# A weight stream with five raw buffers instead of four, smaller tile pools, and three kinds of work pinned to their places in the order

## The chip, the cores and the metric

The kernel runs on one core of one Trainium2 chip. A core has TensorE (PE in the profile; its weight loads are PEld), VectorE (DVE), ScalarE (ACT), GpSimd (POOL) and SyncE (SP), which each take their own instructions in order and wait for each other by semaphores. DMAs are issued from SyncE, GpSimd and ScalarE and run on 16 DMA engines. The metric is device microseconds of one execution. The kernel before takes 915.2 us (median of three, 913.45 to 915.28).

## The reference

One layer of a hybrid transformer block for 512 latent tokens of width 1024, with 256 context tokens as a prefix, all in float32. What it computes, cut to what matters here:

```python
sh1, sc1, g1, sh2, sc2, g2 = split(silu(c) @ w_ada + b_ada, 6)      # modulation from c
hx = rms_norm(x, norm1_g) * (1 + sc1) + sh1
u, vs, q, r, ga, gb, k, v, lr = split(hx @ w_in, IN_SPLITS)
a  = spatial_gating(gelu(u), gelu(vs), ...)                          # 8 groups of 128x128 over chunks of tokens
o  = gla_bidir(q, k, v, lr, ..., states of the context)              # chunked linear attention, 4 heads, 2 directions
ob = rms_norm per head(o) * gla_norm_g * silu(r)
merged = sigmoid(ga) * (a @ w_br_a) + sigmoid(gb) * (ob @ w_br_b)
x  = x + g1 * (merged @ w_o)
hx2 = rms_norm(x, norm2_g) * (1 + sc2) + sh2
a, val = split(hx2 @ w_up, 2)
x  = x + g2 * ((gelu(depthwise_conv3x3(a) + b) * val) @ w_down)
return rms_norm(x, final_norm_g)
```

`r`, `ga`, `gb` and the products with `w_br_a`, `w_br_b` and `w_o` are 512x1024 by 1024x1024.

## The kernel before, in words

**Arithmetic.** A float32 product is made of three products of rounded parts: a weight `raw` is loaded from HBM (512 KB, L238, SyncE), its rounded part `wh` is a copy on ScalarE (L250) and the rest `wl = raw - wh` a subtraction on VectorE (L251). Activations are split in the same way. TensorE then runs `wh` by the high part, `wh` by the low part and `wl` by the high part into one sum.

**The weight stream.** All big weights are pieces of one list, `specs`, used in order by `weights()`. Each use splits up to two pieces ahead (`stream_split(i + 2)`) and loads up to `AHEAD` pieces beyond that one (`stream_load(i + 1 + AHEAD)`). `raw` tiles rotate through `RAW` buffers. A load waits until the `wl` subtraction that read its buffer last is done. `wh` and `wl` have five buffers each, and ScalarE waits for the matmuls that read them last.

**The gate stage.** The three gates and the product with `w_br_a` (`gate`, `gate_product`, L1347) compute a 2x2 block product with seven products instead of eight; each product takes two pieces of the stream and 24 matmuls. Some of the pieces are sums or differences of weight quarters. These sums are made in HBM by GpSimd: `sums_build` issues copies (L215) and accumulating DMAs (L217), one step per `next()`; the `hook()` of the heads and the context products advance it. Each such DMA depends on `after`, the last instruction traced before it, of whatever engine.

**The modulation vectors** `g1`, `sh2`, `sc2`, `g2` come late and by VectorE: `ada2` loads 256 KB pieces of `w_ada` (L1200, SyncE, tiles `wa` of one pool) and adds each, scaled by one element of silu(c) per partition, into `acc` (L1204). Each set is a generator in `bg`; `tick()` advances it at the places that the list `ticks` gives. The loads run `ahead` pieces before the additions.

**The operands of the w_br_a product.** `a_prep` loads eight quarters of the spatial-gating output back from HBM (16 DMAs on SyncE, L1442, tiles `aq`) and makes seven operands, each split by ScalarE (L1448) and VectorE (L1449); `a_step(n)` advances it n steps. `ob_step` does the like for the operand of `w_br_b`.

**What sets the order.** The code is traced in the order it is written, and a scheduler then puts each engine's instructions in an order of its own from its costs and from priorities, within data dependencies and buffer reuse. `in_order(start, engines...)` overrides this: it chains the instructions traced since `start` on the named engines in the order traced. `behind_last(f, engines...)` runs `f()` and chains what it traced behind the instruction of that engine that was traced last; in the kernel before it is used in the channel mixer only. Tiles come from pools: `late` (`LATE` slots of 2 KB per partition), `heap` (`HEAP` slots), and `wp` for the weight stream; a tile in a reused slot waits for the last reader of the one before.

Of the kernel before, what the change touches and what calls it, by code (L numbers as in the profile page):

```python
# [13 lines left out]
ALU = mybir.AluOpType  # L14
AX = mybir.AxisListType

P = 128
# [7 lines left out]
GW = 64  # L25
EPS = 1e-6
O_U, O_VS, O_Q, O_R, O_GA, O_GB, O_K, O_V, O_LR = 0, 1024, 2048, 2560, 3584, 4608, 5632, 6144, 7168
HEAP = 44
LATE = 27
AHEAD = 3  # L30
BLOCKS = 5
TAIL = FT - 4 * BLOCKS
LEAD = 5
# [1 line left out]
SUMS0 = 84  # L35
# [1 line left out]
DENSE = 10  # L37
SHSC = 6
WT = (1, 1)
RAW = 4  # L40


@with_exitstack
def backbone_kernel(
# [7 lines left out]
    V, A, G, T = nc.vector, nc.scalar, nc.gpsimd, nc.tensor  # L52

    cp = stack.enter_context(tc.tile_pool(name="cp", bufs=1))
    wp = stack.enter_context(tc.tile_pool(name="wp", bufs=5))
    hp = stack.enter_context(tc.tile_pool(name="hp", bufs=HEAP))
    lp = stack.enter_context(tc.tile_pool(name="lp", bufs=LATE))
# [11 lines left out]
    def heap(shape, dt=F32, s="h"):  # L69
        return hp.tile(shape, dt, tag="h", name=nm(s))  # L70

    def late(shape, dt=F32, s="l"):
        return lp.tile(shape, dt, tag="l", name=nm(s))
# [13 lines left out]
    dma = nc.sync.dma_start  # L87

    def traced():
        return nc.cur_bb.bb.instructions  # L90

    def in_order(start, *engines):

        last = {}
        for i in traced()[start:]:
            e = i.engine
            if e in engines:
                if e in last:
                    tc.add_manual_dep(i, last[e], mybir.DependencyInfo(
                        mybir.DependencyClass.NoSync, mybir.DependencyReason.DATA), reason="in_order")  # L100
                last[e] = i.name
# [56 lines left out]
    R_AT = len(specs)  # L158
# [17 lines left out]
    quarter, sums = quarters(ffn_w_down[0], 0), sum_tiles(BLOCKS)  # L176
# [29 lines left out]
    def sums_build(quarter, sums):  # L206
        for step in (((0, (0, 1)), (1, (1, 1)), (2, (1, 0)), (3, (0, 1))), ((0, (0, 0)), (3, (1, 1))),
                     ((1, 0),), ((2, 1),)):
            for b in range(len(sums)):
                for dst, src in step:  # L210
                    ap = quarter(b, *src) if isinstance(src, tuple) else sums[b][src]
                    after = traced()[-1]
                    start = len(traced())
                    if len(step) == 4:
                        G.dma_start(sums[b][dst], ap)  # L215
                    else:
                        G.dma_start(sums[b][dst], ap, accum_op=ALU.add)  # L217
                    for i in traced()[start:]:
                        if i.engine == G.engine:
                            tc.add_manual_dep(i, after.name, mybir.DependencyInfo(  # L220
                                mybir.DependencyClass.Sync, mybir.DependencyReason.SCHED_ONLY), reason="sums_build")
                    yield

    def gate_sums():
        for z in gate_weights:
            yield from sums_build(*z)

    building = [(SUMS0, sums_build(quarter, sums)), (2, gate_sums())]

    raws, splits = {}, {}  # L230
    pos = [0, 0, 0]
# [123 lines left out]
    cin = tok_load(ctx[0], 2, late)  # L355
    in_order(START, nc.sync.engine)


    bg = []

# [89 lines left out]
    cs = const([P, KT, 32], "cs")  # L450
# [303 lines left out]
    for k in range(1, KT):  # L754
        g = max(i for i in range(NG) if G0[i] <= k)
# [255 lines left out]
    hooked = [0]  # L1011

    def hook():
        hooked[0] += 1
        if hooked[0] % 2 and 2 < pos[2] < R_AT:
            next(building[1][1], None)
        if hooks:
            f = hooks.pop(0)
            f[0](*f[1:])
# [54 lines left out]
    for t in range(2):  # L1074
        ps = mm()
        for k in range(KT):
            wh, wl = fv[k // 2][1:]
            ah, al = hc[k]
            for i, (a, b) in enumerate(((ah, wh), (ah, wl), (al, wh))):
                T.matmul(ps, a[:, t * P:(t + 1) * P], b[:, k % 2, :], start=(k == 0 and i == 0),  # L1080
                         stop=(k == KT - 1 and i == 2))
            if t and k % 2:
                next(building[1][1])
        v_out(4 + t, ps)
        if t == 0:
            lrp = gl()
            for k0 in (0, 4):
                lr_part(lrp[:, :LC], fc, k0)
            lsc = heap([P, LC], s="lsc")
            A.copy(lsc, lrp[:, :LC])  # L1090
# [25 lines left out]

    ones_r = const([P, P], "ones_r", F32R)
    V.tensor_copy(ones_r, ones)
    sw = [late([P, 4, P], s="sw") for _ in range(2)]
    swT = [heap([P, 4, P], s="swT") for _ in range(2)]  # L1120
    for i in range(2):
        dma(sw[i], sgu_w[0, 4 * i:4 * i + 4].rearrange("g p q -> p g q"))
    sgb = [heap([P, 4, P], s="sgb") for _ in range(2)]
    for i in range(2):
        dma(sgb[i], sgu_b[0:1, 4 * i:4 * i + 4, :].rearrange("o g p -> o (g p)").to_broadcast([P, 512]))

    def sgu_turn(i):
        ps = gl()
        for g in range(4):
            T.transpose(ps[:, g * P:(g + 1) * P], sw[i][:, g, :], ident)  # L1130
        V.tensor_copy(swT[i], ps)

        sgu_hl.append(split_act(swT[i].rearrange("p g q -> p (g q)"), s="sw", lo_pool=late, hi_pool=late, eng=A.copy))
# [18 lines left out]
    def vs_done(hf, t, ps):  # L1152
        vraw[hf][t] = (late if hf else heap)([P, 512], s="vr")
        A.activation(vraw[hf][t], ps, AF.Gelu)

        for h_, t_ in ((), ((), ((0, 0), (0, 1), (1, 0), (1, 1)), ((0, 2), (0, 3), (1, 2)), ((1, 3),))[t])[hf]:
            V.bn_stats(stats[:, t_, h_, :], vraw[h_][t_])
        if hf and t == 0:
            behind.append(len(traced()))
        if hf and t == 1:  # L1160
            in_order(behind.pop(), V.engine)
# [13 lines left out]
    for hf in range(2):  # L1175
        for t in range(4):
            z = vraw[hf][t]
# [6 lines left out]
    def ada2(*kinds, ahead=ADA2):  # L1184
        todo = [(kind, j) for kind in kinds for j in range(2)]
        at = lambda kind, j: 2048 + ("g1", "sh", "sc", "g2").index(kind) * 1024 + j * 512
        acc = []
        for kind, j in todo:
            a_ = late([P, 512], s="acc")
            A.mul(a_.rearrange("p (b r) -> p b r", b=4), ident.unsqueeze(1).to_broadcast([P, 4, P]), 0.0)  # L1190
            c0 = at(kind, j)
            dma(a_[0:1, :], b_ada[0:1, c0:c0 + 512])
            acc.append(a_)
        coming, steps_ = [], [(k, i) for k in range(KT) for i in range(len(todo))]
        for n in range(len(steps_) + ahead):
            if n < len(steps_):
                k, i = steps_[n]
                c0 = at(*todo[i])
                w_ = late([P, 512], s="wa2")
                dma(w_, w_ada[0, k * P:(k + 1) * P, c0:c0 + 512])  # L1200
                coming.append(w_)
            if n >= ahead:
                k, i = steps_[n - ahead]
                V.scalar_tensor_tensor(acc[i], coming.pop(0), cs[:, k, 0:1], acc[i], op0=ALU.mult, op1=ALU.add)  # L1204
            yield
        pairs = []
        for a_ in acc:
            pairs.append(split_act(a_, s="acc", eng=A.copy))
            yield
        yield  # L1210
        yield
        for (ah, al), (kind, j) in zip(pairs, todo):
            ps = gl()
            T.matmul(ps, ones_r, ah, start=True, stop=False)
            T.matmul(ps, ones_r, al, start=False, stop=True)
            if kind in ("g1", "g2"):
                t_ = late([P, 512], s=kind)
                A.copy(t_, ps)
                bc_g[kind, j] = t_
            else:  # L1220
                t_ = heap([P, 4, P], s="dg")
                V.tensor_tensor(t_, ps.rearrange("p (b r) -> p b r", b=4),
                                ident.unsqueeze(1).to_broadcast([P, 4, P]), op=ALU.mult)
                if kind not in cols:
                    cols[kind] = const([P, 8], "col_" + kind)
                V.reduce_sum(cols[kind][:, j * 4:j * 4 + 4], t_, axis=AX.X)
            yield
# [245 lines left out]
    a_steps = a_prep()  # L1473

    def a_step(n):
        for _ in range(n):
            next(a_steps, None)

    ob, ob_step = restores(ob_kept, "ob")

# [9 lines left out]

    def bra_step(i):
        a_step((2, 0, 0, 0, 0, 0, 0)[i])
        if i > 3:
            ob_step()

    a_sum = of_sums(lambda name, b: found.pop((name, b)))
# [287 lines left out]

    n, todo = [0], []

    def behind_last(f, *engines):
        ends = [max(i for i, z in enumerate(traced()) if z.engine == e.engine) for e in engines]
        f()
        for e, i in zip(engines, ends):  # L1790
            in_order(i, e.engine)

    def product_in(ps, t, c0, n_, z, first, last):
        (wh, wl), (ah, al) = z
        for kk in range(2):
# [76 lines left out]
    ends = []  # L1872
# [42 lines left out]
```

## Time and profile before

| | us |
|---|---|
| median of three runs | 915.2 |
| the profiled execution | 916.71 |
| its span | 915.0 |
| TensorE busy | 897.1 (98%) |
| VectorE busy | 716.5 (78%) |
| ScalarE busy | 466.1 (51%) |
| GpSimd busy | 94.1 (10%) |
| one cast of a weight, L250 (178 of them) | 1.052 |
| one subtraction, L251 (178) | 1.220 |
| one modulation addition, L1204 (64) | 0.748 |

The profiled execution took 916.71 us from outside; its span, on which all times of the trace are counted, is 915.0. TensorE is busy almost throughout, so the table says where the others have room, and only a view in order of time says where TensorE waits. In the timeline a row has the start, the length, the engine, the line, the operation and the tiles (out<-in); "x2" merges two. In the chain of waits a row has the start, the length and what the end of the program was waiting for in that time.

### The profile page before, as it was taken

The numbers are of one execution on the slowest core, as the hardware profiler recorded it, in microseconds if no ns is written. First come the engines' busy times: TensorE is split into PE (matmuls) and PEld (weight loads), VectorE is DVE, ScalarE is ACT, GpSimd is POOL, SyncE is SP. The second block draws the span as 40 slices with busy tenths as digits, with TensorE's granted clock in tenths as the row PEclk, the third lists the DMA queues.
The fourth block names the chain that finished last, engine by engine and source line by source line (L and its number), as shares of the span: only waits on it lengthen the run. The fifth ranks groups of instructions, "written<-read, shape, count | busy, mean of one in ns | idle before, by whom it ended". The sixth has DMA issues, their size and how long they took to land.

```text
span 915.0 us, 12469 instructions
## 1 busy us (share of the span) xinstructions
PE 897.1 (98%) x4476; PEld 745.6 (81%) x4476; DVE 716.5 (78%) x1195; ACT 466.1 (51%) x768; POOL 94.1 (10%) x146
## 2 busy tenths in 40 slices
PE   7999999999999999999999999999999999999996
PEld 5778888888888877887888889888888888888885
DVE  5478687779785567659898767898899988986996
ACT  6356465657542636668541537443333434366663
POOL 1300012122112210000000000021111000000000
PEclk9999999999999999999999999999999999999999
DMA  9973677899797999895997850899998632355542
GB/s 284 335 249 117 204 159 134 245 275 249 158 271 250 312 275 310 282 302 180 365 390 263 287 179 24 247 264 275 209 209 199 139 94 95 119 173 187 168 155 92
DMA packets 155931, 199.52 MB, mean 218 GB/s; under 512 B 9257, under 2 KB 88437, under 8 KB 155869
## 3 DMA queue, kind: packets, MB, share of 16 engines
q1 hardware_dynamic: 130765, 136.60, 46.2%
q0 software_dynamic: 23264, 58.95, 27.2%
q10 hardware_dynamic: 1840, 3.18, 0.9%
q8 instruction: 35, 0.57, 0.2%
q14 instruction: 27, 0.22, 0.1%
HBM read 190.31 MB, written 62.91 MB: 277 GB/s over the span
## 4 chain that ended last, share of the span: by engine, by line
PE 89%; DMA 5%; DVE 3%; ACT 1%; issue 1%; SPq 0%; ACTq 0%; DVEq 0%
PE mm L385 33%; PE mm L403 16%; PE gl L1799 9%; PE mm L1347 6%; PE gl L918 3%; PE mm L682 2%; PE gl L1347 2%; DMA wa<-in_w_ada_dram 2%; PE gl L403 2%; DVE wl L251 2%; PE mm L1799 1%; PE gl L682 1%; DMA raw<-in_w_in_dram 1%; PE mm L1030 1%; PE mm L1080 1%; PE gl L591 1%
## 5 line engine op out<-in xcount | busy, mean ns | idle before, releaser
L250 ACT CAST wh<-raw 128x1024 fp32r<-128x1024 f32 x178 | 186.4, 1052 | 200.1 <-PE mm L385 90.5
L251 DVE TENSOR_TENSOR wl<-raw,wh 128x1024 fp32r<-128x1024 f32 x178 | 215.8, 1220 | 65.9 <-ACT wh L250 61.9
L385 PE MATMUL mm<-h2h,wh 128*128 128x512 f32 (+1 forms) x344 | 133.0, 387 | 0.0
L385 PE MATMUL mm<-h2l,wh 128*128 128x512 f32 (+1 forms) x344 | 133.0, 387 | 0.0
L385 PE MATMUL mm<-h2h,wl 128*128 128x512 f32 (+1 forms) x344 | 133.0, 387 | 0.0
L1635 DVE SCALAR_TENSOR_TENSOR cacc<-ca,ccol,cacc 128x441 f32<-128x441 f32 (+2 forms) x176 | 121.8, 695 | 4.3
L385 PEld LDWEIGHTS mm<-h2l,wh 128*128 128x128 f32 x344 | 64.6, 188 | 13.2
L385 PEld LDWEIGHTS mm<-h2h,wh 128*128 128x128 f32 x344 | 64.6, 188 | 13.1
L385 PEld LDWEIGHTS mm<-h2h,wl 128*128 128x128 f32 x344 | 64.6, 188 | 13.0
L1204 DVE SCALAR_TENSOR_TENSOR acc<-wa,cs,acc 128x512 f32<-128x512 f32 x64 | 45.8, 748 | 14.1 <-DMA wa<-in_w_ada_dram 14.1
L1799 PE MATMUL gl<-wh,dal 128*128 128x512 f32 x120 | 46.7, 389 | 0.0
L1799 PE MATMUL gl<-wh,dah 128*128 128x512 f32 x120 | 46.7, 389 | 0.0
L1799 PE MATMUL gl<-wl,dah 128*128 128x512 f32 x120 | 46.7, 389 | 0.0
L1636 ACT ACTIVATE cacc<-cacc 128x512 f32<-128x512 f32 x22 | 13.9, 632 | 55.2 <-DVE cacc L1635 55.2
L385 PE MATMUL mm<-hxh,wh 128*128 128x512 f32 x104 | 41.3, 397 | 0.0
L385 PE MATMUL mm<-hxl,wh 128*128 128x512 f32 x104 | 40.6, 390 | 0.0
L385 PE MATMUL mm<-hxh,wl 128*128 128x512 f32 x104 | 40.5, 390 | 0.0
L215 POOL DMA_DIRECT2D sum<-in_ffn_w_down_dram x20 | 11.4, 570 | 244.7 <-DVE wl L251 150.1
L217 POOL DMA_DIRECT2D sum<-sum x26 | 24.1, 976 | 119.1 <-PE mm L385 43.7
L403 PE MATMUL mm<-wh,hxh 128*128 128x512 f32 x88 | 34.7, 395 | 0.0
L403 PE MATMUL mm<-wl,hxh 128*128 128x512 f32 x88 | 34.4, 390 | 0.0
L403 PE MATMUL mm<-wh,hxl 128*128 128x512 f32 x88 | 34.3, 390 | 0.0
(479 smaller groups left out, 2053.7 us busy)
## 6 DMA issues: line engine op xcount, KB each, us to landing
raw<-sum SPq DMA_DIRECT2D x52, 512.0 KB
wa<-in_w_ada_dram SPq DMA_DIRECT2D x96, 256.0 KB
raw<-in_w_in_dram SPq DMA_DIRECT2D x46, 512.0 KB
raw<-in_ffn_w_up_dram SPq DMA_DIRECT2D x44, 512.0 KB
sum<-in_w_in_dram POOLq DMA_DIRECT2D x36, 512.0 KB, 7.1
sum<-in_ffn_w_down_dram POOLq DMA_DIRECT2D x30, 512.0 KB, 6.5
sum<-sum POOLq DMA_DIRECT2D x26, 512.0 KB, 8.0
raw<-in_ffn_w_down_dram SPq DMA_DIRECT2D x17, 512.0 KB
```

The source lines that it names most:

```text
L217: G.dma_start(sums[b][dst], ap, accum_op=ALU.add)
L250: A.copy(wh, raw)
L251: V.tensor_tensor(wl, raw, wh.bitcast(F32), op=ALU.subtract)
L385: T.matmul(ps, a[:, k, :], b[:, c0:c0 + n], start=(k == 0 and i == 0), stop=(k == KT - 1 and i == 2))
L403: T.matmul(ps, a[:, t * P:(t + 1) * P], b[:, k % 2, :], start=(k == 0 and i == 0), stop=(k == KT - 1 and i == 2))
L682: T.matmul(fps[i], a, b, start=(k == 0 and z == 0), stop=(k == KT - 1 and z == 2))
L918: T.matmul(ps, p_, q_, start=(start and z == 0), stop=(stop and z == 2))
L1204: V.scalar_tensor_tensor(acc[i], coming.pop(0), cs[:, k, 0:1], acc[i], op0=ALU.mult, op1=ALU.add)
L1347: T.matmul(banks[t], a(kk, t), w[:, kk, :], start=(first and b == 0 and kk == 0 and i == 0), stop=(b == 1 and kk == 1 and i == 2), skip_gr ...
L1635: V.scalar_tensor_tensor(o, a_[:, r0 + dy:r1 + dy, c0 + dx:c1 + dx], wcol(tap), o, op0=ALU.mult, op1=ALU.add)
L1636: A.activation(acc, acc, AF.Gelu)
L1799: T.matmul(ps, a, w[:, kk, c0:c0 + n_], start=(first and kk == 0 and i == 0), stop=(last and kk == 1 and i == 2), skip_group_check=True)
```

## The change

Six edits. (1) `RAW` goes from 4 to 5 and `AHEAD` from 3 to 4; the room of the fifth buffer comes from one slot less in each pool (`HEAP` 43, `LATE` 26). (2) In `ada2` the addition into `acc` is made through `behind_last` on VectorE, so that it has its place behind the VectorE instruction traced last. `behind_last` itself moves up to where `ada2` can see it. (3) `a_step` runs its steps through `behind_last` on VectorE. (4) In `sums_build` a DMA depends on the last TensorE instruction traced, and the sums of the gate weights start with the stream's piece 1 instead of 2, are advanced by the hook also at the first pieces, and get two more steps in the context's v product. (5) The loads of the spatial-gating weights and biases are made at a later place (`sgu_load`), and `swT` tiles are taken when they are written. (6) `ob_step` in the w_br_a product starts one product earlier.

```diff
-HEAP = 44
-LATE = 27
-AHEAD = 3
+HEAP = 43
+LATE = 26
+AHEAD = 4
...
-RAW = 4
+RAW = 5
...
 def sums_build(quarter, sums):
...
-                    after = traced()[-1]
+                    after = next(z for z in reversed(traced()) if z.engine == T.engine)
...
-    building = [(SUMS0, sums_build(quarter, sums)), (2, gate_sums())]
+    building = [(SUMS0, sums_build(quarter, sums)), (1, gate_sums())]
...
+    def behind_last(f, *engines):
+        ends = [max(i for i, z in enumerate(traced()) if z.engine == e.engine) for e in engines]
+        f()
+        for e, i in zip(engines, ends):
+            in_order(i, e.engine)
...
 def hook():
-        if hooked[0] % 2 and 2 < pos[2] < R_AT:
+        if hooked[0] % 2 and pos[2] < R_AT:
             next(building[1][1], None)
...
-            if t and k % 2:
+            if k % (2 if t else 4) == (1 if t else 3):
                 next(building[1][1])
...
-    sw = [late([P, 4, P], s="sw") for _ in range(2)]
-    swT = [heap([P, 4, P], s="swT") for _ in range(2)]
-    for i in range(2):
-        dma(sw[i], sgu_w[0, 4 * i:4 * i + 4].rearrange("g p q -> p g q"))
-    sgb = [heap([P, 4, P], s="sgb") for _ in range(2)]
...
+    sw, swT, sgb = [], [], []
+
+    def sgu_load():
+        for i in range(2):
+            sw.append(late([P, 4, P], s="sw"))
+            dma(sw[i], sgu_w[0, 4 * i:4 * i + 4].rearrange("g p q -> p g q"))
...
         if hf and t == 0:
+            sgu_load()
             behind.append(len(traced()))
...
 def ada2(*kinds, ahead=ADA2):
...
-                V.scalar_tensor_tensor(acc[i], coming.pop(0), cs[:, k, 0:1], acc[i], op0=ALU.mult, op1=ALU.add)
+                behind_last(lambda: V.scalar_tensor_tensor(acc[i], coming.pop(0), cs[:, k, 0:1], acc[i],
+                                                           op0=ALU.mult, op1=ALU.add), V)
...
 def a_step(n):
-        for _ in range(n):
-            next(a_steps, None)
+        behind_last(lambda: [next(a_steps, None) for _ in range(n)], V)
...
 def bra_step(i):
-        if i > 3:
+        if i > 2:
             ob_step()
```

The change shifts line numbers: L1204 becomes L1214, L1335 L1346, L1442 L1453, L1233 L1244.

**VectorE, early in the gate stage.** The rows before, from the subtraction of 304.40 in the trace on (`wl<-raw,wh` is a subtraction; `acc<-wa,cs,acc` a modulation addition of the set g1; `dc` and `obt` belong to the gate's output):

```order
L251 TENSOR_TENSOR wl_3491<-raw_3442,wh_3490 128x1024
L1204 SCALAR_TENSOR_TENSOR acc_3444<-wa_779_3450,cs,acc_3444 128x512
L1204 SCALAR_TENSOR_TENSOR acc_3447<-wa_783_3459,cs,acc_3447 128x512
L251 TENSOR_TENSOR wl_3500<-raw_3457,wh_3499 128x1024
L1204 SCALAR_TENSOR_TENSOR acc_3444<-wa_789_3496,cs,acc_3444 128x512
L1204 SCALAR_TENSOR_TENSOR acc_3447<-wa_793_3505,cs,acc_3447 128x512
L251 TENSOR_TENSOR wl_3537<-raw_3494,wh_3536 128x1024
L1204 SCALAR_TENSOR_TENSOR acc_3444<-wa_799_3542,cs,acc_3444 128x512
L251 TENSOR_TENSOR wl_3546<-raw_3503,wh_3545 128x1024
L1204 SCALAR_TENSOR_TENSOR acc_3447<-wa_803_3551,cs,acc_3447 128x512
L251 TENSOR_TENSOR wl_3591<-raw_3540,wh_3590 128x1024
L251 TENSOR_TENSOR wl_3598<-raw_3549,wh_3597 128x1024
```

Now, from the same subtraction on:

```order
L251 TENSOR_TENSOR wl_3507<-raw_3450,wh_3506 128x1024
L251 TENSOR_TENSOR wl_3543<-raw_3465,wh_3542 128x1024
L251 TENSOR_TENSOR wl_3551<-raw_3502,wh_3550 128x1024
L251 TENSOR_TENSOR wl_3595<-raw_3510,wh_3594 128x1024
L251 TENSOR_TENSOR wl_3601<-raw_3546,wh_3600 128x1024
L1346 TENSOR_TENSOR dc_3582<-mm_3401,dt_3441 128x512
```

The six additions between these subtractions are gone from here. They stand, with the other ten of the set, further on, from the subtraction that served the matmul of 348.06 in the trace before:

```order
L251 TENSOR_TENSOR wl_3775<-raw_3730,wh_3774 128x1024
L1214 SCALAR_TENSOR_TENSOR acc_3452<-wa_780_3458,cs,acc_3452 128x512
L251 TENSOR_TENSOR wl_3814<-raw_3736,wh_3813 128x1024
L1214 SCALAR_TENSOR_TENSOR acc_3455<-wa_784_3467,cs,acc_3455 128x512
L251 TENSOR_TENSOR wl_3823<-raw_3770,wh_3822 128x1024
L1214 SCALAR_TENSOR_TENSOR acc_3452<-wa_790_3504,cs,acc_3452 128x512
```

One addition follows one subtraction, in the order of the trace of the code.

**SyncE, ahead of the sixteen operand loads.** Before (`sum_154` and `sum_158` are pieces of the last gate, `aq<-kept` the operand loads):

```order
L238 DMA raw_4172<-in_w_in_dram 128x2x512
L238 DMA raw_4224<-in_w_in_dram 128x2x512
L238 DMA raw_4230<-sum_154 128x2x512
L1442 DMA aq_4138<-kept_3066 128x256
L1442 DMA aq_4138<-kept_3115 128x256
```

and behind the sixteenth of them

```order
L1442 DMA aq_4159<-kept_3372 128x256
L1442 DMA aq_4159<-kept_3387 128x256
L238 DMA raw_4286<-sum_158 128x2x512
L238 DMA raw_4292<-in_w_in_dram 128x2x512
L238 DMA raw_4337<-in_w_in_dram 128x2x512
```

Now, ahead of the first:

```order
L238 DMA raw_4168<-in_w_in_dram 128x2x512
L238 DMA raw_4174<-in_w_in_dram 128x2x512
L238 DMA raw_4226<-sum_154 128x2x512
L238 DMA raw_4232<-sum_158 128x2x512
L1453 DMA aq_4140<-kept_3074 128x256
```

The load of `sum_158`, which was issued behind the sixteen, is now ahead of them.

**GpSimd, the sums of w_br_a.** Before, copies and stores of the spatial-gating output (`kept<-ug`) mix:

```order
L1233 DMA kept_3066<-ug_2971 128x512
L217 DMA sum_157<-sum_156 256x512
L215 DMA sum_159<-in_w_br_a_dram 256x512
L1233 DMA kept_3115<-ug_3042 128x512
L215 DMA sum_165<-in_w_br_a_dram 256x512
L215 DMA sum_160<-in_w_br_a_dram 256x512
```

Now:

```order
L217 DMA sum_157<-sum_156 256x512
L215 DMA sum_159<-in_w_br_a_dram 256x512
L215 DMA sum_160<-in_w_br_a_dram 256x512
L215 DMA sum_161<-in_w_br_a_dram 256x512
L215 DMA sum_162<-in_w_br_a_dram 256x512
L215 DMA sum_163<-in_w_br_a_dram 256x512
L215 DMA sum_164<-in_w_br_a_dram 256x512
L1244 DMA kept_3074<-ug_2977 128x512
```

The last sum of the gates and six of the eight copies of w_br_a now stand ahead of the first store. TensorE's order differs in a few dozen rows, among the heads and behind the gate stage; its products in that stage stand as before.

More of the change, by code (lines that the diff above doesn't have):

```diff
@@ L1118, in backbone_kernel @@
     V.tensor_copy(ones_r, ones)
-    sw = [late([P, 4, P], s="sw") for _ in range(2)]
-    swT = [heap([P, 4, P], s="swT") for _ in range(2)]
-    for i in range(2):
-        dma(sw[i], sgu_w[0, 4 * i:4 * i + 4].rearrange("g p q -> p g q"))
-    sgb = [heap([P, 4, P], s="sgb") for _ in range(2)]
-    for i in range(2):
-        dma(sgb[i], sgu_b[0:1, 4 * i:4 * i + 4, :].rearrange("o g p -> o (g p)").to_broadcast([P, 512]))
+    sw, swT, sgb = [], [], []
[3 more added lines that the diff above has]
+            dma(sw[i], sgu_w[0, 4 * i:4 * i + 4].rearrange("g p q -> p g q"))
+        for i in range(2):
+            sgb.append(heap([P, 4, P], s="sgb"))
+            dma(sgb[i], sgu_b[0:1, 4 * i:4 * i + 4, :].rearrange("o g p -> o (g p)").to_broadcast([P, 512]))
     def sgu_turn(i):
@@ L1130, in sgu_turn @@
             T.transpose(ps[:, g * P:(g + 1) * P], sw[i][:, g, :], ident)
+        swT.append(heap([P, 4, P], s="swT"))
         V.tensor_copy(swT[i], ps)
@@ L1785, in backbone_kernel @@
     n, todo = [0], []
[L1787 to L1791, printed above, removed]
     def product_in(ps, t, c0, n_, z, first, last):
```

## The prediction

> **What bounds the kernel now.** I read the page's busy shares first, then the windows of 50 us (TensorE's busy time stands second, clock, DMA share and GB/s last).
>
> ```profile
> span 915.0 us, 12469 instructions
> PE 897.1 (98%) x4476; PEld 745.6 (81%) x4476; DVE 716.5 (78%) x1195; ACT 466.1 (51%) x768; POOL 94.1 (10%) x146
> ```
>
> ```profile
> 300.00:350.00 50.00, 47.59 (x204) 37.69 (x203) 33.49 (x48) 25.83 (x34) 9.51 (x12) 1.00 1.05 296
> 350.00:400.00 50.00, 49.21 (x229) 40.08 (x228) 32.96 (x36) 32.59 (x44) 0.00 (x0) 1.00 0.91 293
> ```
>
> TensorE sets the time at a clock of 1.00, so the change can win only what TensorE stands still. Both of these windows have holes, 2.4 and 0.8 us, and lie in the gate stage (L1347). Its whole loss follows from the chain of waits, in order of time (start, length, what):
>
> ```profile
> 299.14 5.46 PE mm L1347 x24
> ...
> 309.61 10.31 DMA wa<-in_w_ada_dram
> ...
> 326.53 11.50 DMA raw<-in_w_in_dram
> ```
>
> ```profile
> 397.99 6.23 DMA raw<-sum
> ...
> 425.51 4.16 PE mm L1347 x17
> 430.60 5.44 PE gl L1347 x24
> 436.05 16.32 PE mm L1347 x72
> 452.37 5.44 PE gl L1347 x24
> 457.81 5.44 PE mm L1347 x24
> 463.25 6.80 PE mm L403 x30
> ```
>
> ```profile
> 376.58 0.60 PE L1323 MATMUL gl<-ident,obt 128*128 128x128 f32 x4
> ```
>
> ```profile
> L1323 PE MATMUL gl<-ident,obt 128*128 128x128 f32 x32 | 4.8, 271 | 0.0
> ```
>
> From 299.14 to 463.25 are 164.1 us. They hold four gates of seven products, each of 24 matmuls, 5.44 us where nothing disturbs (0.23 a matmul): 28 x 5.44 = 152.3. The 32 transpositions start (0.60 - 0.27) / 3 = 0.11 us apart: 3.5. The gap from 425.51 + 4.16 to 430.60, 0.9, is four small matmuls of the modulation. That is 156.7, so **7.4 us** are lost. The timelines of TensorE, VectorE and SyncE show how (a bracket has the idle time before and what ended it):
>
> ```profile
> 334.46 0.50 PE L1347 MATMUL mm<-wl,hxh 128*128 128x512 f32 x1 [0.76 <-DVE wl L251]
> 348.06 0.50 PE L1347 MATMUL gl<-wl,xs 128*128 128x512 f32 x1 [1.02 <-DVE wl L251]
> 425.51 0.50 PE L1347 MATMUL mm<-wl,ah 128*128 128x512 f32 x1 [1.19 <-DVE wl L251]
> ```
>
> ```profile
> 312.15 1.22 DVE L251 TENSOR_TENSOR wl<-raw,wh 128x1024 fp32r<-128x1024 f32 x1
> 320.01 0.75 DVE L1204 SCALAR_TENSOR_TENSOR acc<-wa,cs,acc 128x512 f32<-128x512 f32 x1 [6.64 <-DMA wa<-in_w_ada_dram]
> 320.69 2.35 DVE L251 TENSOR_TENSOR wl<-raw,wh 128x1024 fp32r<-128x1024 f32 x2
> ```
>
> ```profile
> 313.40 8.90 SPq L238 DMA_DIRECT2D raw<-sum  x2
> ```
>
> At 313.37 VectorE reaches a modulation step (L1204) whose operand, asked for at 309.61, takes 10.31 us. It stands 6.64 us, and the subtraction behind it starts at 320.69. That subtraction frees a raw buffer: with four, the fourth load after it waits for it. So of the two loads in the SyncE row the second goes only after 320.69 + 1.2 = 321.9; its weight is split just before 334.46, and TensorE stands. The loads behind are as late (326.53 plus 11.50), and TensorE stands again, at 348.06 too. One wait of 6.64 us is paid over several products.
>
> The stall at 425.51 is apart. By its bracket the matmul before ended at 424.32 and, at 0.39 us, began at 423.93; the next was due 0.23 later: 1.35 lost. The other group then holds 7.4 - 1.35 = **6.0**.
>
> ```profile
> 386.59 11.30 SPq L1442 DMA_DIRECT2D aq<-kept  x16
> ```
>
> ```profile
> 405.39 1.23 DVE L251 TENSOR_TENSOR wl<-raw,wh 128x1024 fp32r<-128x1024 f32 x1 [5.15 <-ACT wh L250]
> ```
>
> ```profile
> 405.39:425.45 20.06, 20.06 (x28) 1.00 0.58 195
> ```
>
> Sixteen operand loads hold SyncE from 386.59 to 397.89. The raw load behind them goes at 397.99, whenever its buffer came free. VectorE idles 5.15 us, is then full for 20.06 us, and the last subtraction in that stretch is the one TensorE waits for.
>
> **The change part by part.** *Fifth raw buffer, one load further ahead.* No instruction is added; a load waits for the fifth subtraction before it.
>
> ```profile
> L250 ACT CAST wh<-raw 128x1024 fp32r<-128x1024 f32 x178 | 186.4, 1052 | 200.1 <-PE mm L385 90.5
> ```
>
> The load of 321.9 now waits for 312.15 + 1.22 = 313.4. Even with the longest transfer of the chain it lands at 324.9; cast 1.05, subtraction 1.22 and 0.4 between them give 327.6. The bracket of 334.46 puts the matmul before at 333.2, so the subtraction was due at 333.4: 5.8 us of cover. At 386.6 one more raw load goes ahead of the sixteen. At 386.6 + 11.5 + 2.7 = 400.8 its subtraction is done, before 406.6: 5.8 us earlier, inside the 5.15 of idle.
>
> *Modulation steps pinned.* The g1 set has 16, in windows of that line alone:
>
> ```profile
> 304.00:325.00 21.00, 4.42 (x6) 1.00 1.05 305
> ...
> 349.00:372.00 23.00, 7.28 (x10) 1.00 0.97 320
> ```
>
> In the new order the first stands behind the subtraction for the matmul of 348.06, the others behind one subtraction each after it. The operand asked for at 309.61 is so read after 348, and 10.31 us hide. The subtraction of 320.69 runs when its cast is done, at 315 to 316. The work moves to where VectorE has room:
>
> ```profile
> 335.00:405.00 70.00, 45.07 (x55) 1.00 0.95 296
> ```
>
> Ten of the 16 are in these 45.07 us already; with six more at 0.7 it is 49.3 of 70. Without that room the six would cost 4.4 us.
>
> *Branch operands pinned (a_step).* Of the 28 operations in the full 20.06 us the first subtraction and what follows it now start 4 to 5 us earlier; the last was 1.35 late. Cost: a subtraction can now stand behind an operand that has not landed. The raw load set ahead of the sixteen takes one of the lanes they use in turn, so some of them wait for its landing. Bounds: 0, and 11.50 - 6.23 = 5.3 if that landing is as slow as the worst against what the row at 397.99 took. The DMA share of 0.58 is nearer to the quick row: 1 to 2 us, inside the 4 to 5.
>
> *Sums tied to TensorE, and begun earlier.* No DMA is added: for w_br_a 8 copies and 8 accumulations as before. The last accumulation was issued at
>
> ```profile
> 345.51 0.88 POOL L217 DMA_DIRECT2D sum<-sum  x1 [14.78 <-DMA sum<-sum]
> ```
>
> By the matmuls they are tied to, the copies now go some 40 us earlier and the last accumulation near 310. In 300 to 345 the DMA queues were:
>
> ```profile
> q0 software_dynamic: 2499, 5.72, 56.3%
> q1 hardware_dynamic: 3960, 7.55, 48.8%
> ```
>
> GpSimd's queue, the sums (q0), took more of the engines than the loads (q1). A raw load took 11.50 us there and 6.23 at 397.99, where no sum runs. The loads at 313 to 345 should land nearer 6 than 11; I need only that they get no slower.
>
> A rule speaks against this part. The Trainium skill ("DMA: Bandwidth & Descriptors", section "Issuing engines are not separate DMA queues") says that transfers started by any engine share the same 16 DMA engines, so a sum that is moved presses on whatever runs where it goes. The trace agrees that sharing costs, 11.50 us against 6.23; by the rule the loss would move to 229 to 299 us rather than go, and the time would be A's.
>
> *Smaller pools, later SGU loads, ob_step a product earlier.* I followed each reused slot to its last reader at its old time. Closest is a head's decay chain, which in the new order takes its slot behind a scan product about 5 us later:
>
> ```profile
> 134.61 0.68 DVE L913 TENSOR_TENSOR mx<-kq,mx 128x512 f32<-128x512 f32 x1
> ```
>
> ```profile
> 139.67 1.93 PE gl L953 x16
> ```
>
> Its room to the scores is 139.67 - 135.29 = 4.4 us. Bounds: 0, and 0.6 for each of three heads; I take 0, since VectorE's other work there yields.
>
> *Sum.* Of the 6.0 I take 5.1 (a product beside transpositions or a restart runs a little long even without a wait), of the 1.35 I take 1.3: **6.4 us**. The span becomes 908.6 and the profiled execution of 916.71 becomes 910.3. The median of the runs shown is 915.2, 1.5 below that execution; taken from it: **908.8**.
>
> **The rivals.** *(A) Contention keeps part.* Earlier loads and sums put more transfers in flight where the DMA share is 1.05 and 0.91. If half of the 6.0 stays: 915.2 - 1.3 - 3.0 = 910.9, and up to 913 with the late operands' 2. For it: 11.50 against 6.23. Against: 5.8 us of cover even at 11.50. Chance 0.18.
>
> *(B) The loads do not come earlier.* SyncE issues in order, and modulation loads stand among the raw loads; one that waits for its slot would hold the raw load behind it, whatever the buffers. Then it stays at 914.5 to 915.5. Against it: the row of two raw loads over 8.90 us ends with the buffer's release. Chance 0.07.
>
> *(C) A pinned operation holds VectorE; slower.* Place: the operands after 386, and the second modulation set at 440 to 458, whose loads stand behind raw loads on SyncE. Price: before, 6.64 us of standing cost 6.0. The subtraction
>
> ```profile
> 448.15 1.22 DVE L251 TENSOR_TENSOR wl<-raw,wh 128x1024 fp32r<-128x1024 f32 x1
> ```
>
> is due a quarter into the product of 452.37, at 453.7: 4.3 us of room. What VectorE stands beyond that is paid one for one, so the change loses from 4.3 + 6.4 + 1.8 = 12.5 us at one place, or from two standings like the one of 6.64: 915.2 - 6.4 + 2 x 6.0 = 920.8. I say 917 to 921. For it: 10.31 and 11.50 us occur. Against: a share of 0.58 at 405 to 425. Chance 0.10.
>
> **How the numbers follow.** Forecast 0.65, A 0.18, B 0.07, C 0.10. The forecast's own range is 907.5 (all 7.4 and a little) to 910.3 (4.9). To hold 8 in 10 I reach over A: 907.0 to 913.3. About 0.2%, 1.8 us, is what a measurement of this kernel can tell from no change. Faster is the forecast and A, 0.83; same is B, 0.07; slower is C, 0.10.
>
> **What would show it.** Right: no modulation step on VectorE from 304 to 335 and no idle of 6.64; the raw load of 321.9 at about 313; TensorE 50.00 in 300 to 350 with a DMA share below 1.0 and q0 far under 56.3%; one raw load ahead of the sixteen, VectorE's idle before 405 under 2 us, no bracket near 425; a gate stage of about 157.5 us. Raw loads at 313 to 345 that still take near 11 us would mean that the sums were not what made them long. Wrong: new brackets at L1347 behind a pinned step or operand (C), the same holes with raw loads as late as before (B), or holes among the heads, before 230 us (pools).

## The result, and the profile after

| | before | after |
|---|---|---|
| median, us | 915.2 (913.45 to 915.48, five runs) | 910.56 (909.77 to 911.14, five runs) |
| the profiled execution, us | 916.71 | 910.56 |
| its span, us | 915.0 | 908.9 |
| gate stage, us | 164.2 | 157.3 |

The ratio is 0.9944, with a 95% interval of 0.9932 to 0.9957: 4 to 6 us faster. The gate stage is counted here, and for every experiment, from the start of its first product's first matmul to the start of the first matmul behind its last product.

The windows of 50 us of the kernel after, which answer to the two shown before:

```profile
300.00:350.00 50.00, 50.00 (x222) 41.37 (x222) 35.07 (x48) 30.15 (x40) 5.67 (x7) 1.00 0.96 276
350.00:400.00 50.00, 50.00 (x237) 41.27 (x236) 33.38 (x38) 33.79 (x45) 0.00 (x0) 1.00 0.89 304
```

TensorE is full in both, and its list of waits between 290 and 470 us is empty. The chain of waits in that stage has only TensorE's products left:

```profile
299.97 5.46 PE mm L1358 x24
305.43 5.44 PE gl L1358 x24
310.87 16.32 PE mm L1358 x72
327.19 5.44 PE gl L1358 x24
...
354.39 0.44 PE gl L1334 x4
354.83 5.50 PE mm L1358 x24
...
451.78 5.44 PE mm L1358 x24
457.22 12.92 PE mm L409 x57
```

Here 24 matmuls take 5.44 us, as in the undisturbed pieces before, and 5.50 where they stand next to transpositions (L1334). VectorE no longer stands at a modulation step; its timeline over the place of the 6.64 us reads

```profile
310.63 1.23 DVE L251 TENSOR_TENSOR wl<-raw,wh 128x1024 fp32r<-128x1024 f32 x1 [2.32 <-ACT wh L250]
312.47 1.23 DVE L251 TENSOR_TENSOR wl<-raw,wh 128x1024 fp32r<-128x1024 f32 x1 [0.61 <-ACT wh L250]
316.07 1.22 DVE L251 TENSOR_TENSOR wl<-raw,wh 128x1024 fp32r<-128x1024 f32 x1 [2.37 <-ACT wh L250]
322.00 1.23 DVE L251 TENSOR_TENSOR wl<-raw,wh 128x1024 fp32r<-128x1024 f32 x1 [4.70 <-ACT wh L250]
```

and SyncE's, there and at the sixteen operand loads,

```profile
311.88 2.22 SPq L238 DMA_DIRECT2D raw<-sum  x2
```

```profile
379.14 1.72 SPq L238 DMA_DIRECT2D raw<-sum  x2
380.92 10.23 SPq L1453 DMA_DIRECT2D aq<-kept  x16
391.25 0.91 SPq L238 DMA_DIRECT2D raw<-in_w_in_dram  x2
```

The pair of loads whose second went at 321.9 is out by 314.1. But VectorE still idles 4.70 us before 322.00, behind a cast whose weight is late, because the transfers have not become short. The DMA issues from 300 to 345 us of the kernel after:

```profile
q1 hardware_dynamic: 4495, 8.56, 57.3%
q0 software_dynamic: 1604, 3.37, 37.6%
...
raw<-sum SPq DMA_DIRECT2D x8, 512.0 KB, 7.3
raw<-in_w_in_dram SPq DMA_DIRECT2D x6, 512.0 KB, 12.1
sum<-sum POOLq DMA_DIRECT2D x4, 512.0 KB, 11.0
...
sum<-in_w_br_a_dram POOLq DMA_DIRECT2D x1, 512.0 KB, 9.4
```

Six of the fourteen loads still take a median of 12.1 us, the other eight 7.3 (the last number of a row is the median from issue to landing). Five accumulations are left there (the last two rows), and the last of them is issued at

```profile
320.06 0.87 POOL L217 DMA_DIRECT2D sum<-sum  x1 [5.13 <-DMA sum<-sum]
```

and not near 310, since each waits for the one before it to land. So the loads were not all made quick; they are asked for earlier.

### The profile page after: what moved, and what is told of

It is laid out like the page before. It is cut to its first block, busy times and chain, and to the rows that moved or that the text cites. A ratio compares the mean times of both kernels' runs of the same rounds, so it can differ in the third digit from the quotient of the medians.

```text
span 908.9 us, 12461 instructions
## 1 busy us (share of the span) xinstructions
PE 894.3 (98%) x4476; PEld 745.9 (82%) x4476; DVE 717.3 (79%) x1195; ACT 466.8 (51%) x768; POOL 93.2 (10%) x146
## 4 chain that ended last, share of the span: by engine, by line
PE 96%; DVE 1%; ACT 1%; DMA 0%; issue 0%; ACTq 0%
PE mm L391 33%; PE mm L409 15%; PE mm L1358 12%; PE gl L1803 9%; PE gl L1358 5%; PE gl L924 3%; PE mm L688 2%; PE gl L409 2%; PE mm L1803 1%; PE gl L688 1%; PE mm L1036 1%; PE mm L1086 1%; PE gl L597 1%; PE gl L959 1%; PE gl L1250 1%; PE mm L561 1%
## 5 line engine op out<-in xcount | busy, mean ns | idle before, releaser
L1214 DVE SCALAR_TENSOR_TENSOR acc<-wa,cs,acc 128x512 f32<-128x512 f32 x64 | 45.8, 746 | 0.0
L1646 ACT ACTIVATE cacc<-cacc 128x512 f32<-128x512 f32 x22 | 13.9, 632 | 52.4 <-DVE cacc L1645 52.3
```

The source lines that it names most:

```text
L1214: behind_last(lambda: V.scalar_tensor_tensor(acc[i], coming.pop(0), cs[:, k, 0:1], acc[i], op0=ALU.mult, op1=ALU.add), V)
L1646: A.activation(acc, acc, AF.Gelu)
```

## The experiments

In the rows of the kernels below VectorE has the modulation steps and the subtractions where the edit says, so the edits can be taken apart there; elsewhere the scheduler's order can differ a little, as a wait among the heads that only e5 has suggests. The kernel before ran beside each of them; the ratios are against those runs, in which its median was 916.4 to 916.5, 1.2 to 1.3 us above that of the five runs in the first table.

| | median us | lowest to highest | ratio to before, 95% | gate stage us |
|---|---|---|---|---|
| e1 four buffers | 913.1 | 911.07 to 916.44 | 0.9972 (0.9959 to 0.9986) | 159.3 |
| e2 steps free | 915.32 | 913.28 to 919.32 | 0.9989 (0.9976 to 1.0003) | 163.9 |
| e3 sums as before | 910.63 | 909.79 to 911.17 | 0.9942 (0.9929 to 0.9955) | 157.8 |
| e4 steps pinned alone | 914.32 | 912.75 to 917.5 | 0.9981 (0.9965 to 0.9997) | 160.4 |
| e5 buffer and steps | 910.89 | 910.17 to 911.27 | 0.9938 (0.9925 to 0.9951) | 157.3 |
| e6 a_step free | 909.8 | 908.87 to 911.04 | 0.9929 (0.9915 to 0.9943) | 157.3 |
| e7 HEAP 44, LATE 25 | 910.86 | 910.56 to 911.66 | 0.9938 (0.9924 to 0.9953) | 157.3 |
| e8 before again, one run | 915.03 | | | 163.2 |
| e9 before, copies only | 909.12 | 908.96 to 909.56 | 0.9922 (0.9898 to 0.9945) | 157.3 |
| e10 e1, copies only | 909.99 | 909.89 to 910.33 | 0.9931 (0.9911 to 0.9951) | 157.3 |
| e11 the change again | 909.98 | 909.51 to 910.85 | 0.9931 (0.9915 to 0.9947) | 157.3 |
| e12 e6 again | 910.06 | 909.0 to 910.79 | 0.9931 (0.9913 to 0.9949) | 157.3 |

**e1 and e2: the two edits that should matter, each undone.**

```diff
 # e1, against the changed kernel
-HEAP = 43
-LATE = 26
-AHEAD = 4
-RAW = 5
+HEAP = 44
+LATE = 27
+AHEAD = 3
+RAW = 4
 # e2, against the changed kernel
-                behind_last(lambda: V.scalar_tensor_tensor(acc[i], coming.pop(0), cs[:, k, 0:1], acc[i],
-                                                           op0=ALU.mult, op1=ALU.add), V)
+                V.scalar_tensor_tensor(acc[i], coming.pop(0), cs[:, k, 0:1], acc[i], op0=ALU.mult, op1=ALU.add)
```

> The changed kernel with edit 1 undone (RAW 4, AHEAD 3, HEAP 44, LATE 27); the rest of the change stays. Theory (the stalls of the gate stage come from a modulation step that holds VectorE for 6.64 us, and the fifth buffer is a second cover for the same thing): with the step pinned elsewhere the subtraction of 320.69 runs at 315 to 316, so the load behind it goes at about 316.5 instead of 321.9 and, at 11.5 us, its subtraction is done at 330.7 against 333.4 due. The first group of stalls stays away but for 0 to 1.5 us; one raw load falls back behind the sixteen operand loads, which can bring 0 to 1 us of the stall near 425 back. 0 to 2.5 us slower than the changed kernel, 911 to 913. Rival (the buffers are what pays, pinning only reorders): the 6 us come back, 914 to 916.

> The changed kernel with edit 2 undone: the 16 modulation steps of g1 are where the scheduler puts them, six of them between the subtractions at 304 to 321 as in the kernel before. Theory: VectorE stands some 6 us at about 314 again, but each load is released one subtraction earlier, so only the loads behind the standing are late; and the step near 352 holds a subtraction again. 1 to 3 us slower than the changed kernel, 911.5 to 913.5. Rival 1 (the standing is the only cause): all 6 us come back, 915 to 916. Rival 2 (the fifth buffer alone covers it): within 0.6 us of the changed kernel.

e1 is 2.5 us slower than the change's 910.56, a hair past what the theory gave (913.1 against 911 to 913). e2 is 4.8 us slower: more than its theory gave, and inside the 915 to 916 of rival 1. Its ratio to the kernel before reaches 1.0003, so the fifth buffer and the other edits without the pinned steps can't be told from no change. Neither edit is enough without the other. TensorE's rows with waits in e1, then in e2:

```profile
329.48 0.49 PE L1358 MATMUL gl<-wh,xs 128*128 128x512 f32 x1 [0.65 <-ACT wh L250]
330.74 0.50 PE L1358 MATMUL gl<-wl,xs 128*128 128x512 f32 x1 [0.77 <-DVE wl L251]
```

```profile
323.48 0.50 PE L1357 MATMUL mm<-wl,xs 128*128 128x512 f32 x1 [1.84 <-DVE wl L251]
327.30 0.50 PE L1357 MATMUL mm<-wl,xs 128*128 128x512 f32 x1 [2.17 <-DVE wl L251]
```

In e1 no modulation step stands in the way, and yet a weight comes late. Its load on SyncE and its cast on ScalarE, which waited for the transfer:

```profile
312.16 0.38 SPq L238 DMA_DIRECT2D raw<-in_w_in_dram  x1
```

```profile
328.38 1.05 ACT L250 CAST wh<-raw 128x1024 fp32r<-128x1024 f32 x1 [1.09 <-DMA raw<-in_w_in_dram]
```

Asked for at 312.16, landed at 328.3: 16 us, the longest step in e1's chain of waits there. A raw buffer comes round in transfer, cast and subtraction, about 16 + 2.7 us; four of them would then give a weight every 4.7 us (an estimate, as if every transfer were as long), and TensorE takes one in 2.72 (5.44 for two). By the same arithmetic five give one in 3.7, still slower, and yet the change's stage had no wait: the stream has one more weight in hand, and not every transfer is that long. In e2 the steps stand behind operands again, and the fifth buffer did not cover it:

```profile
321.53 0.75 DVE L1214 SCALAR_TENSOR_TENSOR acc<-wa,cs,acc 128x512 f32<-128x512 f32 x1 [4.33 <-DMA wa<-in_w_ada_dram]
```

Here the standings are several (3.70, 1.45, 1.16, 4.33 and 1.93 us in a row), not one of 6.64, and the last holds the subtraction that TensorE is already waiting for, so an earlier load is of no use to it.

**e3: the sums where they were.**

```diff
-                    after = next(z for z in reversed(traced()) if z.engine == T.engine)
+                    after = traced()[-1]
...
-    building = [(SUMS0, sums_build(quarter, sums)), (1, gate_sums())]
+    building = [(SUMS0, sums_build(quarter, sums)), (2, gate_sums())]
...
-        if hooked[0] % 2 and pos[2] < R_AT:
+        if hooked[0] % 2 and 2 < pos[2] < R_AT:
...
-            if k % (2 if t else 4) == (1 if t else 3):
+            if t and k % 2:
```

> The changed kernel with edit 4 undone: the sums of the gate weights depend on the last instruction traced of any engine and start one step later, so that accumulations for w_br_a run until about 350 as before. Theory (cover makes landings of 11 to 14 us harmless; in the changed kernel's trace loads of this stage still take a median of 12.1 us): within 0.8 us of the changed kernel, 910 to 911.4. Rival (sums that contend with the loads were part of the loss): 2 to 3 us slower, 912.5 to 913.5.

910.63: the change's time. GpSimd's queue is back at 55.8% of the DMA engines in 300 to 345 (the change: 37.6%), and the stage at 157.8 us has 0.4 more. With the other edits in place, where the sums run makes no difference to the median that can be measured. The rival is out.

**e4 and e5: one edit, and two, on the kernel before.** e4 is the second diff above turned round, with `behind_last` moved up; e5 has the first as well.

> The kernel before with edit 2 alone: the modulation steps pinned, four buffers, everything else as before. Theory: the first group of stalls (6.0 us by the trace of before) goes but for 0 to 1.5, the stall near 425 (1.35) stays: 4 to 5 us faster than before by trace, 910.5 to 911.5 as span plus 1.7; against the runs' median 910.5 to 912. Rival (needs the fifth buffer): under 2 us faster, above 913.5.

> The kernel before with edits 1 and 2 alone (fifth buffer, modulation steps pinned); sums, a_step, SGU loads and ob_step as before. Theory (these two are the whole gain; either alone leaves 2.5 to 4.5 us of stalls): a median of 910.1 to 911.3, as the changed kernel, gate stage 157.2 to 158.3 us. Rival (a_step pinned is needed against the stall near 425): about 1.3 us slower than the changed kernel, with a bracket of 1 us at L1347 near 420.

e4's one profile has a span of 910.9 and a stage of 160.4, a gain of 4.1 us as the theory said; but that was the fastest of its nine runs (912.75), the others go up to 917.5, and its median of 914.32 is the rival's: under 2 us faster by the ratio, and above 913.5. e5 is the whole gain, 910.89, with every run within 1.1 us. So edits 1 and 2 together are what pays. In the gate stage edits 3, 4 and 6 and the moved SGU loads (5) add nothing: 157.3 us with them and without. Over the whole kernel e5 is 0.3 us above the change's first runs and 0.9 above its later ones (e11); 0.4 of the latter is a wait of TensorE among the heads that e5's profile has and e11's has not, and whether an edit takes it away was not tested.

**e6 and e12: the operand steps free.**

```diff
-        behind_last(lambda: [next(a_steps, None) for _ in range(n)], V)
+        for _ in range(n):
+            next(a_steps, None)
```

> The changed kernel with edit 3 undone: the operand steps of the w_br_a product are where the scheduler puts them. Theory (the fifth buffer already takes the raw load ahead of the sixteen operand loads): within 0.6 us of the changed kernel, 910 to 911.2. Rival (the pinned places are what saves the 1.35 us near 425): 911.5 to 912.2.

> Experiment e6 again (operand steps free). Theory: its 909.8 was the scatter of the heads and the start; within 0.6 us of the changed kernel beside it. Rival: it beats the changed kernel by 0.5 to 1 us again.

909.8, then 910.06 beside 909.98 of the change (e11). Pinning a_step is worth nothing, and leaving it free is not a better kernel either: the 0.8 us by which e6 lies below the change's first runs did not come again.

**e7: the room of the fifth buffer taken from one pool.**

```diff
-HEAP = 43
-LATE = 26
+HEAP = 44
+LATE = 25
```

> The changed kernel with the room of the fifth buffer taken from the late pool alone: HEAP 44, LATE 25. Theory (the wait for a scan product by the decay chain's tile, a tile of the heap pool, is the stall of 0.45 us at 132.78): that stall goes, 0.2 to 0.5 us faster than the changed kernel, 910.0 to 910.4. Rival (the scheduler's order there, not the slot): the same stall, the same time. A late tile that is now short would show as a new wait and 1 us or more slower.

The only place among the heads where the change made TensorE wait is the decay chain. TensorE's row in the change, and in e7:

```profile
132.78 0.51 PE L924 MATMUL gl<-st,qh 128*128 128x256 f32 x2 [0.29 <-DVE mx L876]
```

```profile
168.19 0.51 PE L924 MATMUL gl<-st,qh 128*128 128x256 f32 x2 [0.77 <-DVE mc L844]
```

The first lost 0.45 us against the usual step. e7 has it no more, as the theory said, but has the second, which lost 0.93, and the median of 910.86 misses the 910.0 to 910.4 that the theory gave. `mx` is a tile of the heap pool and `mc` one of the late pool, so a slot moved from one pool to the other seems to move the wait; VectorE was busy just before both tiles, so the slot is not shown to be what set their place.

**e8: the kernel before again.**

> The kernel before, unchanged, profiled once more. Theory (its executions differ, 913 to 919 us, because the gate stage's stalls differ from run to run): the span less the gate stage's excess over 156.7 us is 907.0 to 908.3 as in the first profile (915.0 less 7.4), whatever the span. Rival (the spread lies elsewhere, in the start or the clock): the gate stage is 164 us again and the rest differs.

```profile
423.82 0.50 PE L1347 MATMUL mm<-wl,ah 128*128 128x512 f32 x1 [2.24 <-DVE wl L251]
```

This execution took 915.03 us, and its stage 163.2, with a different share of stalls: 2.40 us lost here at what was 425.51, and less ahead of it. 913.3 less the 6.5 of the stage's excess over 156.7 is 906.8, just below the range that the theory gave (the first profile: 915.0 less 7.5, 907.5). So of the 1.7 us between the two executions 1.0 lies in the stage, and 0.7 ahead of it; two executions settle little between the theory and its rival.

**e9 and e10: the accumulations left out.**

```diff
-    def sums_build(quarter, sums):
+    def sums_build(quarter, sums, copies_only=False):
...
-                    else:
+                    elif not copies_only:
                         G.dma_start(sums[b][dst], ap, accum_op=ALU.add)
...
-            yield from sums_build(*z)
+            yield from sums_build(*z, copies_only=z is gate_weights[-1])
```

> The kernel before, with the eight accumulating DMAs of the w_br_a sums left out (the copies stay, so the sums are wrong, and so is the output); VectorE's order is that of the kernel before. It asks whether the transfers of 10 to 14 us are the sums' doing. Theory A (contention is the root: with no accumulation after 306, loads and modulation operands land in 5 to 7 us, the step at 314 waits 2 us at most): the first group of stalls is gone or under 1.5 us, 4 to 5 us faster than before, and the stall near 425 stays. Theory B (the order is the root: the step stands behind its operand whatever the load): still 2 us or more of first-group stalls, under 3 us faster.

> Experiment e1 (four buffers, steps pinned) with the same eight accumulations left out. Theory A and the round trip (a buffer comes round in transfer + 2.7 us; four buffers give one weight per quarter of that, TensorE takes one in 2.72; at 14 us it is 4.2, at 6 us it is 2.2): the stalls of 1.85 us near 330 go, gate stage 157.3 to 157.8. Theory B (four buffers are too few whatever the transfer takes): the stalls stay, 159 or more.

These two say most. e9 has the order of the kernel before on VectorE, four buffers, the steps between the subtractions, and its stage is at 157.3: not one wait of TensorE is left, at 425 too. VectorE at the place of the 6.64 us:

```profile
312.19 0.75 DVE L1204 SCALAR_TENSOR_TENSOR acc<-wa,cs,acc 128x512 f32<-128x512 f32 x1 [1.61 <-DMA wa<-in_w_ada_dram]
...
315.57 0.75 DVE L1204 SCALAR_TENSOR_TENSOR acc<-wa,cs,acc 128x512 f32<-128x512 f32 x1 [1.49 <-DMA wa<-in_w_ada_dram]
```

e10 differs from e1 by the accumulations alone. The DMA issues of e1 between 300 and 345 us, then the queues and issues of e10:

```profile
raw<-sum SPq DMA_DIRECT2D x8, 512.0 KB, 13.9
raw<-in_w_in_dram SPq DMA_DIRECT2D x6, 512.0 KB, 4.6
...
wa<-in_w_ada_dram SPq DMA_DIRECT2D x7, 256.0 KB, 12.9
```

```profile
q1 hardware_dynamic: 5534, 10.52, 76.3%
q0 software_dynamic: 160, 0.52, 2.9%
...
raw<-sum SPq DMA_DIRECT2D x9, 512.0 KB, 4.3
raw<-in_w_in_dram SPq DMA_DIRECT2D x6, 512.0 KB, 3.9
wa<-in_w_ada_dram SPq DMA_DIRECT2D x11, 256.0 KB, 4.7
```

Theory A holds for the first group of stalls in both; that the stall near 425 would stay, as it said of e9, did not come, and e9 gained over 7 us, not 4 to 5. Without the accumulations the median load takes 3.9 to 4.3 us instead of 4.6 and 13.9 (e1), or 10.7 and 14.0 where the accumulations run until about 350 as before (e3), and then neither the steps' place nor the number of buffers matters to the stage. So the stalls need the accumulations; edits 1 and 2 together are a cover against them, and each alone is too short a cover. (The 0.9 us by which e9's median is below e11's lie outside the stage, which takes as long in both: in the two profiles TensorE reaches it 1.7 us sooner in e9, which has no wait at the decay chain.) What was not run: edit 4 alone, which moves part of the accumulations out of this stage and might do with four buffers; and plain copies of as many bytes in the accumulations' place, which would tell what the accumulating itself costs.

## Why the prediction was right, and where it was not

- **What bounds it: right.** TensorE's waits in the gate stage were what could be won. With none left the stage takes 157.3 us; predicted was about 157.5. So 6.9 of the 7.4 us were loss, and the rest is products of 5.50 us next to transpositions, which the prediction allowed for when it took 5.1 of 6.0.
- **The sum of 6.4: near for the span, mis-set on the median.** The span fell 6.1 us, from 915.0 to 908.9: 6.9 in the stage, and 0.8 the other way ahead of it. There TensorE's first matmul came 0.7 later (6.31 against 5.57 us into the span; in e8, the kernel before, it came at 6.35, and in e7, with the change's order, at 5.5, so this is scatter), the decay chain took 0.45, and some 0.4 was gained that was not followed. The profiled execution was predicted at 910.3 and came at 910.56. The median was predicted at 908.8 and came at 910.56: 4.6 us below the 915.2, not 6.4. The step that failed is "taken from it: **908.8**": it took the stall of one execution from the median of others. The 916.71 of that execution was no outlier: the 47 runs of the kernel before beside the experiments have medians of 916.4 to 916.5, and against these the change gains 6.3 us (e11, ratio 0.9931), about the sum. Low were the runs that gave 915.2, 913.45 to 915.48; why is open. A kernel whose stage is at its floor stays near 910 whichever runs it is compared with.
- **The range.** 910.56 lies 0.3 above the forecast's own 907.5 to 910.3 and nearer to A's 910.9 than to 908.8. It lies in the 907.0 to 913.3 because that range reached over A. So the time alone speaks for A as much as for the forecast; that A's mechanism did not come is read from the traces.
- **Fifth buffer: right in its place, mistaken as a cover by itself.** The load of 321.9 went at about 313.7 (predicted 313), TensorE did not wait. That "the longest transfer of the chain", 11.5 us, leaves 5.8 us of cover was too mild: 16 us occur (e1), and with the steps free (e2) all the rest of the change together gains 1.0 us (ratio 0.9989, interval to 1.0003: no gain is possible too).
- **Steps pinned: right.** No step runs between 304 and 335, no idle of 6.64. VectorE had the room (35.07 and 33.38 us busy of 50). Alone it is worth 1.7 us by the ratio (e4), not the 4 to 5 that e4's theory expected of it.
- **Sums moved: the size wrong, the cause underrated.** "Nearer 6 than 11" did not come for all: a median of 12.1 us for six of the loads, 7.3 for the other eight. The last accumulation went at 320.06, not near 310. "I need only that they get no slower" saved the forecast. The DMA share did fall below 1.0 (0.96), the q0 share to 37.6% and not far lower. The rule that was weighed against this part, of the Trainium skill ("DMA: Bandwidth & Descriptors", section "Issuing engines are not separate DMA queues"), is that transfers started by any engine share the same 16 DMA engines. e10 against e1 agrees with it: without GpSimd's accumulations SyncE's loads of sums take 4.3 us instead of 13.9. But the loss did not move to 229 to 299 us, where TensorE is full (50.00 us busy of 200 to 250 and of 250 to 300 after). And the prediction took contention for a rival that keeps part of the loss; the loss needs it (e9), and the other edits cover it.
- **The stall at 425.51: it went, the cause is not shown.** The raw load does stand ahead of the sixteen, VectorE's idles at that place are 1.00 and 1.15 us, no bracket is left, and the operand loads' wait for a raw load's landing cost SyncE 1.3 us, inside the bounds. (The "5.8 us earlier, inside the 5.15 of idle" can't be: 5.8 is more than 5.15.) But in e1, e4, e9 and e10 a load of a sum stands behind the sixteen as before, and the stall is gone as well; a_step free (e6) did not bring it back. So neither "one more raw load ahead" nor the pinned operands can be called what removed it. What the traces do show is when that load goes against TensorE's own progress, counted back from the first of the four small matmuls behind the stalled product:

| | load goes | small matmul | lost at the stall | between, less the loss |
|---|---|---|---|---|
| before | 397.99 | 429.50 | 1.35 | 30.2 |
| e8 | 396.14 | 427.81 | 2.40 | 29.3 |
| e9 | 390.89 | 422.02 | 0 | 31.1 |
| e4 | 393.97 | 425.41 | 0 | 31.4 |
| e10 | 390.76 | 422.58 | 0 | 31.8 |
| e1 | 393.63 | 425.73 | 0 | 32.1 |

The two executions that lose are the two in which the load goes latest, and the later of them loses more. That fits a load that comes too late by a microsecond or two; no run moved it alone, so it stays a reading.

- **Pools at nothing: wrong by 0.45 us**, at one head, within the bound of 0.6 that the prediction kept for it, and in the chain that it named.
- **The rivals.** A's half of 6.0 did not stay: TensorE has no wait in the stage. B did not come. C did not: no pinned step holds a subtraction in the trace after.

## What to carry to other kernels

When an engine in order waits for a DMA ahead of the work that feeds the bottleneck, ask first why the DMA is slow: here, with eight background accumulations left out, the loads of sums landed in 4.3 us instead of 13.9 (e10, e1), and none of the stage's waits, which looked like faults of the order, was left. Compare a buffer's round trip over the number of buffers with what the consumer takes per item, and work it out with the longest transfer that the stage shows: with four it was 4.7 us against 2.72, and TensorE waited. It is a warning and not a bound: with five it was 3.7, and the stage had no wait. And if a kernel's executions scatter, subtract a stall from the execution in which it was read; the fix removes the scatter with the stall, so its gain over a median is smaller where those runs stalled less, and larger where they stalled more.

## What was not expected

The scatter itself. The kernel before ranges over 6 us (913.1 to 919.17 in 26 runs beside e1 to e4), and e1, e2 and e4, which keep some of the stall, over 4.8 to 6.0; every kernel whose stage is at its floor keeps within 2.2 us, though these have 4 to 6 runs each. That the stall makes the scatter is likely by this; the two profiles of the kernel before show only 1.0 of their 1.7 us in the stage. And 512 KB took a median of 3.9 to 4.3 us where no accumulation ran beside it, and 4.6 to 14.0 where some did, though the bytes moved differ less: in 300 to 345 us 246 GB/s in e10, 268 in e1, 296 before. What in an accumulation costs the other transfers so much was not tested.
